# Shared slots of the expert stage gathered ahead of the last own slots

## The chip, the cores and the metric

The kernel runs on one core of one Trainium2 chip. Its engines are TensorE (matmul), VectorE, ScalarE and GpSimd, each with a queue of its own that it works through in order; SyncE issues most plain transfers, GpSimd issues the gathers, whose rows it picks by an index. The metric is the time of one execution in microseconds, as a median of runs.

## The reference

A two-layer network on 256 latent tokens of width 1024 (with 256 context tokens in the first layer). Layer 0 mixes with a state-space scan and attention, layer 1 with a gated MLP; each layer ends with the PEER expert stage, which is what the change touches:

```python
def _peer(h, wq, k1, k2, u_tab, v_tab):
    q = (t @ wq).reshape(n_tok, PEER_HEADS, PEER_DKEY)
    s1 = jnp.einsum('thd,hkd->thk', q[..., :half], k1)
    s2 = jnp.einsum('thd,hkd->thk', q[..., half:], k2)
    ...  # the best 16 of 16384 experts for each of 8 heads: idx, gate
    def expert_block(args):
        tb, ib, gb = args
        act = jax.nn.gelu(jnp.einsum('phkd,pd->phk', jnp.take(u_tab, ib, axis=0), tb), approximate=False)
        return jnp.einsum('phk,phkd->pd', gb * act, jnp.take(v_tab, ib, axis=0))
```

Each token has 128 experts (8 heads x 16). For each it takes the dot product with a row of `u_tab`, a gelu, the gate, and adds that multiple of a row of `v_tab`.

## The kernel before, in words

The 16384 experts are cut into 128 classes of 128. The experts of the first 75 classes (`X`) are computed densely: TensorE multiplies all tokens with every U block (`products`, order "S"), a spread of the gates masks the result `ge`, and then TensorE multiplies `ge` with every V block (order "V", 75 blocks), summing into four PSUM tiles `py`. The blocks come by SyncE into four buffers `wr`, one block of 128 x 1024 floats each. A block of V costs 8 matmuls in the instruction order, which the trace shows as 16 passes.

The experts of the other 53 classes are gathered. The 256 tokens are two tiles (t = 0, 1) of 128. For each tile GpSimd gathers 56 *own slots* (`CAP`): slot s brings, for each of the 128 tokens, one row of 2048 floats (U row and V row, `fetch`, tensor `rows`). VectorE takes the dot product with the token (`dot`, writes `junk` and `act`), ScalarE makes the weight (`weigh`: gelu, then times the gate, `wt`), VectorE adds the weighted V row to `acc`. What tokens have beyond 56 goes to three *shared slots* (`SHARED`): up to 128 pairs of any token and expert each. A shared slot needs two gathers, the expert's row (`in_uv`) and the token's row (`hs`), hence two row buffers; its dot product is taken between them, VectorE makes a 128 x 256 matrix `sc` that carries the weight to the right token, and TensorE multiplies `sc` with the V rows into the same `py` (8 matmuls).

There are six row buffers (`NR`). Two slots stay in `pend` between dot product and accumulation (`LAG`), so up to four gathers are under way. All instructions are written by one Python program: generators for TensorE (`products`), for gathering (`gather`), for the choice and spread (`choose`) and for the end (`ending`) yield to a planner, `schedule`, which runs the one whose engine is free first by the planner's own clock (`clk`). What comes out is a fixed order on each engine; the chip's waits are semaphores between engines. `clock.ready(x)` is the planned time at which `x` is there; `LATE` is how far past it the planner's TensorE clock must be before a shared product is written.

After the last slot, `ending` scales `acc` and adds the residual, `overflow` reads a counter `fi` and branches on it (the branch body, for still longer lists, is not run here), and `finish` (layer 0) or `final` (layer 1) updates x from `py` and `acc`. Every engine goes through the branch. Line 173 is the helper that records all operations, so the profile's groups are told apart by tile names.

Of the kernel before, what the change touches and what calls it, by code (L numbers as in the profile page):

```python
# [33 lines left out]
CAP = 56  # L34
TAKE, TAKES = 24, 3
SHARED = 3
NR = 6
# [14 lines left out]
PACE = 1.0  # L52
NAW = 4
KORDER = (8, 10, 12, 0, 2, 4, 6, 14)
LATE = 6.0
LAG = 2


# [149 lines left out]
def tile_backbone(ctx: ExitStack, tc: tile.TileContext, a: dict, out: bass.AP):  # L208
# [3 lines left out]
    clock = Clock()  # L212
    clk = clock.at
    T, V, S, G, Q = (Engine(e, n, clock) for e, n in ((nc.tensor, "T"), (nc.vector, "V"), (nc.scalar, "S"), (nc.gpsimd, "G"), (nc.sync, "D")))
# [41 lines left out]
    def at(*aps):  # L256

        return lambda: clk["T"] + SLACK >= max(clock.ready(x) for x in aps)
# [1170 lines left out]
    def peer(l, mod, a2, sh2):  # L1429
# [42 lines left out]
        qr, vals, inds = {}, [], []  # L1472
# [152 lines left out]
        def take(t, r_, idx=None, gsl=None):  # L1625

            if idx is None:
                idx, gsl = (x[t][:, TAKE * r_:TAKE * (r_ + 1)] for x in (gidx, gsel))
            tmp = lambda n, dt: q2.tile([P, TAKE], dt, tag=n, name=n)
            ks = [tmp(f"ks{i}", F32) for i in range(3)]  # L1630
            for e in range(0, TAKE, 8):
                for i in range(3):
                    V.max(ks[i][:, e:e + 8], key[t][i])
                for i in range(3):
                    V.match_replace(key[t][i], ks[i][:, e:e + 8], key[t][i], 0.0)
            ki, kb, kc = (tmp(f"k{n}", I32) for n in "ibc")
            for k_, x in ((ki, ks[0]), (kb, ks[1]), (kc, ks[2])):
                V.tensor_copy(k_, x)
            z_, ok, lo = (tmp(n, F32) for n in ("z_", "ok", "lo"))
            V.tensor_scalar(z_, ks[0], 0.0, 65536.0, op0=ALU.is_equal, op1=ALU.mult)  # L1640
            V.tensor_scalar(ok, ks[0], 0.0, None, op0=ALU.is_gt)
            V.tensor_scalar(idx, ki, ROWS - 1, None, op0=ALU.bitwise_and)
            V.tensor_tensor(idx, idx, z_, op=ALU.add)
            V.tensor_scalar(kb, kb, 65535, None, op0=ALU.bitwise_and)
            V.tensor_scalar(kc, kc, 65535, None, op0=ALU.bitwise_and)
            V.tensor_scalar(lo, kc, 1.0 / (GLO * GHI), -32768.0 / (GLO * GHI), op0=ALU.mult, op1=ALU.add)
            V.scalar_tensor_tensor(gsl, kb, 1.0 / GHI, lo, op0=ALU.mult, op1=ALU.add)
            V.tensor_tensor(gsl, gsl, ok, op=ALU.mult)
# [175 lines left out]
        def fetch(rw, idx, src=None, last=(P - X) * P - 1):  # L1824
            G.indirect_dma_start(out=rw, out_offset=None, in_=a[f"uv{l}"] if src is None else src,
                                 in_offset=bass.IndirectOffsetOnAxis(ap=idx, axis=0),
                                 bounds_check=last, oob_is_err=False)

        def weigh(act, g_):
            S.activation(act, act, AF.Gelu)  # L1830
            w = q2.tile([P, 1], F32, tag="wt", name="wt", bufs=4)
            S.activation(w, act, AF.Copy, scale=g_)
            return w
# [65 lines left out]
        def urgent():  # L1899

            if not todo_v:
                return False
            return clk["V"] + SPREAD * todo_v[1] + RUSH > clk["T"] + PTILE * (todo_v[0] + left[0] - 2 * X)

        def gather():
            yield lambda: "sel" in done
            nxt = [clk["T"]]
            todo = [(t, s) for t in range(2) for s in range(CAP)] + [(2, k) for k in range(SHARED)]
            free, work, pend = list(qr["rows"]), [], []
            taken = [EARLY, 0]  # L1910
            head = [0]

            def issue():
                t, s = todo[head[0]]
                if len(free) < (2 if t == 2 else 1):
                    return False
                head[0] += 1
                if t < 2:
                    if s % TAKE == 0 and s // TAKE >= taken[t]:
                        take(t, taken[t])  # L1920
                        taken[t] += 1
                    bufs = [free.pop(0)]
                    fetch(bufs[0], gidx[t][:, s:s + 1])
                else:
                    bufs = [free.pop(0), free.pop(0)]
                    fetch(bufs[0], lidx[:, s:s + 1])
                    fetch(bufs[1][:, 0:D], lidx[:, SHARED + s:SHARED + s + 1], hs, 2 * P - 1)
                work.append((t, s, bufs))
                return True

            def weigh_last():
                if pend and len(pend[-1]) == 5:
                    t, s, bufs, act, g_ = pend[-1]
                    w = weigh(act, g_)
                    if t == 2:
                        sc = q2.tile([P, 2 * P], F32, tag="sc", name="sc")
                        V.tensor_scalar(sc, iotaL[:, :2 * P], spot[:, s, 0:1], w, op0=ALU.is_equal, op1=ALU.mult)
                        w = sc
                    pend[-1] = (t, s, bufs, w)

            def accumulate():
                t, s, bufs, w = pend.pop(0)
                v_ = bufs[0][:, D:2 * D]
                if t == 2:
                    last = s == SHARED - 1 and "pl" in done
                    for t_ in range(2):
                        for n in range(2):
                            mm(py[t_][n], w[:, t_ * P:(t_ + 1) * P], v_[:, n * 512:(n + 1) * 512], False, last)
                    if s == SHARED - 1:
                        done.add("shared")  # L1950
                elif s == 0:
                    V.tensor_scalar(acc[1], v_, w, None, op0=ALU.mult)
                else:
                    V.scalar_tensor_tensor(acc[1], v_, w, acc[1], op0=ALU.mult, op1=ALU.add)
                if t == 0 and s == CAP - 1:
                    Q.dma_start(out=acs, in_=acc[1])
                if t < 2 and s == CAP - 1:
                    done.add(("own", t))
                free.extend(bufs)

            lst = None
            for i in range(NR - LAG):
                issue()
            while work or pend:
                weigh_last()
                if work:
                    t, s, bufs = work.pop(0)
                    if t == 2:
                        yield lambda: "pv" in done
                    yield at(*bufs)  # L1970
                    g_ = lg[:, s, 1:2] if t == 2 else gsel[t][:, s:s + 1]
                    pend.append((t, s, bufs, dot(bufs[1] if t == 2 else h2[t], bufs[0]), g_))
                    if t == 1 and s >= 4:

                        if taken[0] < TAKES or taken[1] < TAKES:
                            t_ = 0 if taken[0] < TAKES else 1
                            take(t_, taken[t_])
                            taken[t_] += 1
                        elif lst is None:
                            lst = listing()  # L1980
                        if lst:
                            next(lst, None)
                if len(pend) > LAG or not work:
                    if len(pend) == 1:
                        weigh_last()
                    if pend[0][0] == 2:
                        yield lambda: clk["T"] >= clock.ready(pend[0][3]) + LATE
                    accumulate()
                while head[0] < len(todo) and len(work) + len(pend) < NR:
                    if todo[head[0]][0] == 2 and todo[head[0]][1] == 0:  # L1990
                        while taken[0] < TAKES or taken[1] < TAKES:
                            t_ = 0 if taken[0] < TAKES else 1
                            take(t_, taken[t_])
                            taken[t_] += 1
                        for _ in lst or listing():
                            pass
                    if not issue():
                        break
                yield
                rest = len(todo) - head[0] + len(work)  # L2000
                nxt[0] = max(nxt[0], clk["T"] - 3.0) + PACE * PTILE * max(0, left[0] - TAIL) / max(1, rest)
                if rest:
                    yield lambda: clk["T"] > nxt[0] and not urgent()
# [170 lines left out]
```

## Time and profile before

| | |
|---|---|
| median of 3 runs | 1990.38 us (1984.54 to 1993.85) |
| profiled execution | 1996.46 us, span 1994.7 us |
| TensorE busy | 1863.6 us |
| VectorE busy | 1369.0 us |
| GpSimd busy | 629.5 us |
| ScalarE busy | 540.2 us |
| mean granted TensorE clock | 0.970 |
| end of the expert stage, layer 0 | first update of x at 1123.83 us |
| end of the expert stage, layer 1 | first update of x at 1980.41 us |

Times in the rows are microseconds from the span's start. In a timeline the columns are start, duration, engine, line, operation, output and inputs, count, and in brackets how long the engine was idle ahead of it and what released it. Rows of several instructions are merged; the start is that of the first. Layer 0 is the first layer, layer 1 the second. `PEld` is TensorE's weight load, which runs beside the matmuls.

### The profile page before, as it was taken

Reading aid. Unit: us, or ns where it says so; the run is one execution under the profiler, and the core shown is the slowest. Engines: PE = TensorE matmul, PEld = TensorE weight load, DVE = VectorE, ACT = ScalarE, POOL = GpSimd, SP = SyncE. Lnnn points to the kernel's source line nnn. Section 1 sums busy time; section 2 is a strip of 40 time slices with the busy share of each in tenths; the row PEclk is TensorE's granted clock in tenths of the full one; section 3 lists DMA queues with packets and bytes.
Section 4 is the critical chain, followed back from the end, with each engine's and each line's share of the span. In section 5 each row is a group of like instructions: output and inputs, shape, how many; then the busy total and the mean of one; then the engine's idle time right before and its main releaser. Section 6 shows DMA issues by size and latency. Waiting matters only on the chain. (4 is left out here: it accounts for less than half of the span.)

```text
span 1994.7 us, 27972 instructions
## 1 busy us (share of the span) xinstructions
PE 1863.6 (93%) x9888; PEld 1539.0 (77%) x9888; DVE 1369.0 (69%) x3376; ACT 540.2 (27%) x1428; POOL 629.5 (32%) x400
## 2 busy tenths in 40 slices
PE   7989999899999999998999698999999999989994
PEld 4666565679988878887878588799888888868773
DVE  4466276546985898778567625479858986876667
ACT  5334344345212222110111354442112221111111
POOL 2324312276010222133322198650112221334222
PEclk9999999899999999999999899999999999989998
DMA  8656766155367989699999474453579885999993
GB/s 314 217 173 220 251 219 212 68 180 169 128 218 276 358 301 365 221 359 367 398 417 395 149 254 147 161 188 128 195 286 362 302 342 220 355 355 400 417 411 128
DMA packets 133064, 529.87 MB, mean 266 GB/s; under 512 B 17941, under 2 KB 18133, under 8 KB 105197
## 3 DMA queue, kind: packets, MB, share of 16 engines
q1 hardware_dynamic: 97440, 301.76, 42.8%
q0 software_dynamic: 34176, 225.07, 28.9%
q8 instruction: 78, 1.28, 0.3%
q10 hardware_dynamic: 1296, 1.16, 0.2%
q14 instruction: 74, 0.61, 0.1%
HBM read 540.28 MB, written 6.91 MB: 274 GB/s over the span
## 5 line engine op out<-in xcount | busy, mean ns | idle before, releaser
L173 POOL DMA_INDIRECT rows<-in_uv,gidx x224 | 270.4, 1207 | 912.9 <-DVE acc L173 657.5
L173 PE MATMUL pb<-wr,ge 128*128 128x256 f32 x2400 | 539.5, 384 | 19.5 <-DMA wr<-in_dn 17.5
L173 PE MATMUL pa<-phf,wr 128*128 128x256 f32 x2400 | 539.1, 385 | 0.0
L173 PEld LDWEIGHTS pb<-wr,ge 128*128 128x128 f32 x2400 | 453.7, 191 | 103.1 <-DMA wr<-in_dn 41.9
L173 PEld LDWEIGHTS pa<-phf,wr 128*128 128x128 f32 x2400 | 458.9, 193 | 61.8
L173 POOL TENSOR_TENSOR whl<-wr,whl 128x1024 fp32r<-128x1024 f32 (+2 forms) x128 | 310.6, 2440 | 306.6 <-ACT whl L173 298.9
L173 DVE SCALAR_TENSOR_TENSOR junk<-rows,h 128x1024 bf16<-128x1024 f32 x224 | 273.8, 1222 | 128.7 <-DMA rows<-in_uv,gidx 128.6
L173 DVE SCALAR_TENSOR_TENSOR acc<-rows,wt,acc 128x1024 f32<-128x1024 f32 x220 | 281.8, 1281 | 0.3 <-ACT wt L173 0.3
L173 ACT ACTIVATE act<-act 128x1 f32<-128x1 f32 x230 | 46.7, 203 | 573.7 <-DVE junk L173 554.8
L173 ACT CAST whl<-wr 128x1024 fp32r<-128x1024 f32 (+2 forms) x136 | 137.3, 1019 | 86.3 <-PE pa L173 37.2
L173 ACT ACTIVATE sg<-pa 128x8 f32<-128x8 f32 (+20 forms) x98 | 26.5, 270 | 278.1 <-PE pa L173 252.3
L173 PE MATMUL pb<-oc,o 128*128 128x75 f16 x1024 | 85.3, 252 | 14.8 <-DVE oc L173 13.6
L173 PE MATMUL pa<-phh,whl 128*128 128x256 f32 x512 | 96.3, 285 | 2.2 <-DVE phf L173 1.5
L173 PEld LDWEIGHTS <-o 128*128 128x128 f16 x1024 | 78.0, 118 | 24.0 <-DVE oc L173 14.8
L173 ACT ACTIVATE ge<-pa 128x256 f32<-128x256 f32 (+18 forms) x146 | 46.9, 321 | 144.9 <-PE pa L173 144.3
L173 PE MATMUL pa<-aw,condT 128*32 128x512 f32 x320 | 78.7, 605 | 6.9 <-DMA aw<-in_ada_w 5.1
L173 PEld LDWEIGHTS pa<-phh,whl 128*128 128x128 f32 x512 | 80.7, 191 | 3.6 <-DVE phf L173 1.9
L173 DVE SCALAR_TENSOR_TENSOR ge<-pb,ge 128x292 f32<-128x292 f32 (+19 forms) x128 | 42.1, 370 | 59.4 <-ACT ge L173 56.5
L173 PE MATMUL pa<-phl,whl 128*128 128x256 f32 x256 | 73.2, 286 | 2.4 <-POOL phl L173 1.3
L173 DVE TENSOR_TENSOR o<-iotaJ,pkT 128x1024 f16<-128x1024 f16 x64 | 43.8, 684 | 36.8 <-PE pb L173 36.8
L173 ACT ACTIVATE wt<-act,gsel 128x1 f32<-128x1 f32 x224 | 66.0, 295 | 7.3
L173 DVE MAX8 ge<-ge 128x8 f32<-128x128 f32 (+1 forms) x192 | 38.4, 254 | 26.0 <-ACT ge L173 25.9
(490 smaller groups left out, 2436.6 us busy)
## 6 DMA issues: line engine op xcount, KB each, us to landing
wr<-in_dn SPq DMA_DIRECT2D x300, 512.0 KB
aw<-in_ada_w SPq DMA_DIRECT2D x164, 256.0 KB
wr<-in_wq SPq DMA_DIRECT2D x32, 512.0 KB
wr<-in_w_out SPq DMA_DIRECT2D x16, 512.0 KB
wr<-in_gm_w_v SPq DMA_DIRECT2D x16, 512.0 KB
wr<-in_gm_w_u SPq DMA_DIRECT2D x16, 512.0 KB
wr<-in_gm_w_out SPq DMA_DIRECT2D x16, 512.0 KB
wr<-in_w_xbc SPq DMA_DIRECT2D x12, 512.0 KB
```

Of the source, the lines that this page charges most:

```text
L173: return f(*args, **kw)
```

## The change

Before, the list of slots is tile 0's 56, tile 1's 56, then the 3 shared ones. After, the 3 shared slots stand ahead of tile 1's last 14 (`AFTER`), that is, ahead of own slots 42 to 55. When a shared slot's turn to be accumulated comes, it goes to a list `lates` and its buffers stay taken; its product is written when TensorE's planned clock is `LATE` = 5.0 (before 6.0) past the planned time of its `sc`, while the loop goes on with other slots. The loop's condition and the count of buffers in use include `lates`.

```diff
-LATE = 6.0
+LATE = 5.0
+AFTER = 14
...
-            todo = [(t, s) for t in range(2) for s in range(CAP)] + [(2, k) for k in range(SHARED)]
-            free, work, pend = list(qr["rows"]), [], []
+            todo = [(t, s) for t in range(2) for s in range(CAP)]
+            todo[2 * CAP - AFTER:2 * CAP - AFTER] = [(2, k) for k in range(SHARED)]
+            free, work, pend, lates = list(qr["rows"]), [], [], []
...
-            def accumulate():
-                t, s, bufs, w = pend.pop(0)
+            def accumulate(t, s, bufs, w):
...
-            while work or pend:
+            while work or pend or lates:
+                if lates and clk["T"] >= clock.ready(lates[0][3]) + LATE:
+                    accumulate(*lates.pop(0))
+                if not work and not pend and lates:
+                    yield lambda: clk["T"] >= clock.ready(lates[0][3]) + LATE
+                    continue
...
-                if len(pend) > LAG or not work:
+                if len(pend) > LAG or not work and pend:
                     if len(pend) == 1:
                         weigh_last()
-                    if pend[0][0] == 2:
-                        yield lambda: clk["T"] >= clock.ready(pend[0][3]) + LATE
-                    accumulate()
-                while head[0] < len(todo) and len(work) + len(pend) < NR:
+                    x = pend.pop(0)
+                    if x[0] == 2:
+                        lates.append(x)
+                    else:
+                        accumulate(*x)
+                while head[0] < len(todo) and len(work) + len(pend) + len(lates) < NR:
```

What this makes of the instruction order is shown for the end of layer 1's expert stage. TensorE before: `wr,ge` are the V blocks (8 rows a block), `rows,sc` the shared products, `fi` the branch.

```order
L173 MATMUL pa<-rhs,cmp 128x2 x6
L173 MATMUL pb<-wr,ge 128x256 x312
L173 MATMUL pb<-rows_13285,sc 128x256 x8
L173 MATMUL pb<-rows_13281,sc 128x256 x8
L173 MATMUL pb<-rows_13283,sc 128x256 x8
L2036 TENSOR_LOAD fi
```

TensorE after, the same place:

```order
L174 MATMUL pa<-rhs,cmp 128x2 x6
L174 MATMUL pb<-wr,ge 128x256 x264
L174 MATMUL pb<-rows_13277,sc 128x256 x8
L174 MATMUL pb<-rows_13279,sc 128x256 x8
L174 MATMUL pb<-wr,ge 128x256 x16
L174 MATMUL pb<-rows_13275,sc 128x256 x8
L174 MATMUL pb<-wr,ge 128x256 x32
L2044 TENSOR_LOAD fi
```

The first two products now stand ahead of the last 6 blocks, the third ahead of the last 4. In layer 0 they stand ahead of the last 9 and the last 7 (`x264`, two products, `x16`, one product, `x56`).

GpSimd before, the end of its gathers in layer 1: `in_uv,gidx` are own slots, `in_uv,lidx` and `hs,lidx` the two gathers of a shared slot.

```order
L173 DMA rows_13283<-in_uv,gidx_11927 128x2048
L173 DMA rows_13284<-in_uv,gidx_11927 128x2048
L173 DMA rows_13285<-in_uv,lidx 128x2048
L173 DMA rows_13286<-hs,lidx 128x1024
L173 DMA rows_13281<-in_uv,lidx 128x2048
L173 DMA rows_13282<-hs,lidx 128x1024
L173 DMA rows_13283<-in_uv,lidx 128x2048
L173 DMA rows_13284<-hs,lidx 128x1024
L2036 TENSOR_LOAD fi
```

GpSimd after, from own slot 41 (buffer 13276) to own slot 47:

```order
L174 DMA rows_13276<-in_uv,gidx_11921 128x2048
L174 DMA rows_13277<-in_uv,lidx 128x2048
L174 DMA rows_13278<-hs,lidx 128x1024
L174 DMA rows_13279<-in_uv,lidx 128x2048
L174 DMA rows_13280<-hs,lidx 128x1024
L174 DMA rows_13275<-in_uv,lidx 128x2048
L174 DMA rows_13276<-hs,lidx 128x1024
L174 DMA rows_13277<-in_uv,gidx_11921 128x2048
L174 DMA rows_13278<-in_uv,gidx_11921 128x2048
L174 DMA rows_13279<-in_uv,gidx_11921 128x2048
L174 DMA rows_13280<-in_uv,gidx_11921 128x2048
L174 DMA rows_13275<-in_uv,gidx_11921 128x2048
```

The three shared slots fill all six buffers, and own slots 42, 44 and 46 are gathered into buffers that TensorE's first, second and third shared product reads (13277, 13279, 13275). Eight more own slots follow.

VectorE after, in the same place, from own slot 41's dot product (`junk,act<-rows_13276,h`) on:

```order
L174 SCALAR_TENSOR_TENSOR junk,act<-rows_13276,h_11913 128x1024
L174 SCALAR_TENSOR_TENSOR acc<-rows_13280,wt,acc 128x1024
L174 SCALAR_TENSOR_TENSOR junk,act<-rows_13277,rows_13278 128x1024
L174 SCALAR_TENSOR_TENSOR acc<-rows_13275,wt,acc 128x1024
L174 TENSOR_SCALAR sc<-iotaL,spot,wt 128x256
L174 SCALAR_TENSOR_TENSOR junk,act<-rows_13279,rows_13280 128x1024
L174 SCALAR_TENSOR_TENSOR acc<-rows_13276,wt,acc 128x1024
L174 TENSOR_SCALAR sc<-iotaL,spot,wt 128x256
L174 SCALAR_TENSOR_TENSOR junk,act<-rows_13275,rows_13276 128x1024
L174 TENSOR_SCALAR sc<-iotaL,spot,wt 128x256
L174 SCALAR_TENSOR_TENSOR junk,act<-rows_13277,h_11913 128x1024
```

The accumulation of own slot 41 (`rows_13276`) stands behind the second shared dot product, and the third shared slot's gathers need the buffer that it frees. Before, the shared dot products came after own slot 55's, and the two passes over `acc` stood ahead of the third.

## Rows read from the trace of the kernel before

**Rows 1.** The page: its span, and busy time of each engine.
```profile
span 1994.7 us, 27972 instructions
PE 1863.6 (93%) x9888; PEld 1539.0 (77%) x9888; DVE 1369.0 (69%) x3376; ACT 540.2 (27%) x1428; POOL 629.5 (32%) x400
```

**Rows 2.** Timeline, layer 1, VectorE's dot products and a weight block's loads.
```profile
1913.45 1.23 DVE L173 SCALAR_TENSOR_TENSOR junk<-rows,h 128x1024 bf16<-128x1024 f32 x1 [1.35 <-DMA rows<-in_uv,gidx]
1917.22 1.23 DVE L173 SCALAR_TENSOR_TENSOR junk<-rows,h 128x1024 bf16<-128x1024 f32 x1 [1.34 <-DMA rows<-in_uv,gidx]
...
1932.40 3.32 PEld L173 LDWEIGHTS pb<-wr,ge 128*128 128x128 f32 x16 [0.41 <-DMA wr<-in_dn]
```

**Rows 3.** Stretches: length; PE, PEld, DVE, ACT, POOL busy; PEclk, DMA share, GB/s.
```profile
1930.00:1940.00 10.00, 9.88 (x45) 7.72 (x43) 6.00 (x8) 1.29 (x5) 2.98 (x3) 1.00 1.02 411
1940.00:1950.00 10.00, 9.38 (x40) 7.31 (x40) 7.11 (x9) 1.49 (x6) 2.02 (x3) 1.00 0.87 333
1950.00:1955.00 5.00, 4.17 (x19) 3.71 (x20) 4.31 (x6) 1.00 (x4) 2.57 (x2) 1.00 0.38 115
...
1960.00:1965.00 5.00, 0.00 (x0) 0.00 (x0) 3.12 (x5) 0.50 (x2) 2.72 (x2) 0.62 0.89 328
```

**Rows 4.** Timeline, the end of layer 1's expert stage.
```profile
1950.69 1.23 DVE L173 SCALAR_TENSOR_TENSOR junk<-rows,h 128x1024 bf16<-128x1024 f32 x1 [0.99 <-DMA rows<-in_uv,gidx]
...
1950.83 5.45 PE L173 MATMUL pb<-wr,ge 128*128 128x256 f32 x24 [1.43 <-DMA wr<-in_dn]
...
1960.06 1.22 DVE L173 SCALAR_TENSOR_TENSOR junk<-rows,h 128x1024 bf16<-128x1024 f32 x1
...
1962.45 0.99 POOL L173 DMA_INDIRECT rows<-hs,lidx  x1 [0.30 <-issue]
1964.37 1.22 DVE L173 SCALAR_TENSOR_TENSOR junk<-rows,rows 128x1024 bf16<-128x1024 f32 x1 [1.89 <-DMA rows<-hs,lidx]
...
1966.72 0.41 DVE L173 TENSOR_SCALAR sc<-iotaL,spot,wt 128x256 f32<-128x256 f32 x1
...
1967.18 12.70 PE L173 MATMUL pb<-rows,sc 128*128 128x256 f32 x48 [10.91 <-DVE sc L173]
...
1968.54 1.23 DVE L173 SCALAR_TENSOR_TENSOR junk<-rows,rows 128x1024 bf16<-128x1024 f32 x1 [1.41 <-DMA rows<-hs,lidx]
...
1971.21 2.48 DVE L173 TENSOR_TENSOR acc<-acc,ge 128x1024 f32<-128x1024 f32 x2
1973.61 1.22 DVE L173 SCALAR_TENSOR_TENSOR junk<-rows,rows 128x1024 bf16<-128x1024 f32 x1
...
1975.43 0.41 DVE L173 TENSOR_SCALAR sc<-iotaL,spot,wt 128x256 f32<-128x256 f32 x1 [0.60 <-ACT wt L173]
...
1975.99 0.15 DVE L173 TENSOR_TENSOR fi<-fi,ff 1x1 int32<-1x1 int32 x1
1979.32 1.28 ACT L173 ACT_TABLE_LOAD   x1 [3.92 <-ACTq L2038]
1980.41 0.69 DVE L173 TENSOR_TENSOR x<-pb,ge 128x512 f32<-128x512 f32 x1 [4.27 <-DMA rows<-hs,lidx]
```

**Rows 5.** Timeline, the end of layer 0's expert stage.
```profile
1058.50 1.23 DVE L173 SCALAR_TENSOR_TENSOR junk<-rows,h 128x1024 bf16<-128x1024 f32 x1 [1.34 <-DMA rows<-in_uv,gidx]
...
1069.68 3.32 PEld L173 LDWEIGHTS pb<-wr,ge 128*128 128x128 f32 x16 [0.44 <-DMA wr<-in_dn]
...
1073.32 1.23 DVE L173 SCALAR_TENSOR_TENSOR junk<-rows,h 128x1024 bf16<-128x1024 f32 x1 [1.04 <-DMA rows<-in_uv,gidx]
...
1077.18 24.04 PEld L173 LDWEIGHTS pb<-wr,ge 128*128 128x128 f32 x112 [0.42 <-DMA wr<-in_dn]
...
1102.86 1.22 DVE L173 SCALAR_TENSOR_TENSOR junk<-rows,h 128x1024 bf16<-128x1024 f32 x1
...
1109.84 13.36 PE L173 MATMUL pb<-rows,sc 128*128 128x256 f32 x48 [8.22 <-DVE sc L173]
...
1123.83 0.69 DVE L173 TENSOR_TENSOR x<-pb,ge 128x512 f32<-128x512 f32 x1 [4.11 <-PE pa L173]
```

## The prediction

> **What bounds the kernel now.** I read the page first, then the timeline of the last 170 us of each layer, the stretch table over the second end, and the instruction order of both programs. The span is 1994.7 us and TensorE is busy for 93% of it [rows 1], so only stretches in which TensorE has nothing to do, or its successor waits, are worth anything. The change touches two: the ends of the two expert stages.
>
> Up to about 45 us before each end, three things run in step. VectorE starts one dot product per own slot, 3.77 us apart (1913.45, 1917.22), each released by the landing of its gather [rows 2]. TensorE starts one block of V weights about as often; its block at 1932.40 takes 3.32 us of loads after a 0.41 us wait for its transfer [rows 2]. A gather (128 x 8 KB) and a weight block (128 x 4 KB) share the transfer engines, which are full: DMA share 1.02 up to 1940 (the 1930 stretch), 0.87 from 1940 to 1950 [rows 3]. Transfers set the pace, and TensorE loses 0.3 to 0.45 us a block to them.
>
> Then the second layer ends like this [rows 4]. TensorE starts its last 24 weight passes at 1950.83 and is through at 1956.28. The last own slot's dot starts at 1960.06 (I number own slots 0 to 55; slot 41, fourteen earlier, starts at 1913.45). Only then come the shared slots: dots at 1964.37, 1968.54, 1973.61. TensorE idles from 1956.28 to 1967.18 and its 48 passes of shared products end at 1979.88; the first update of x starts at 1980.41. VectorE's own work of this end is over at 1976.14. So before, TensorE's late shared products end last, and VectorE has some slack. In the first layer the same: 48 passes from 1109.84, 13.36 us, update at 1123.83 [rows 5].
>
> **The change part by part.** Nothing is added or dropped: 6 shared gathers, 3 dots, 3 `sc` and 24 matmuls a layer are moved ahead of 14 own slots. What counts is who then waits.
>
> *TensorE.* In the new order the first two products stand ahead of the last 6 weight blocks in the second layer (16 + 32 rows, 8 a block), of the last 9 in the first (16 + 56); the third stands two blocks later. One product is 16 passes, like a block: 24.04 us for 112 [rows 5], 3.43 us. [...]
>
> *The ring.* Three shared slots take two buffers each: all six. GpSimd's queue has own slot 42 next, into the first shared slot's buffers, and that instruction waits for TensorE's product; the 13 own gathers queued behind it wait too, VectorE waits for them, and the transfer engines have only weights to carry. Slot 44 waits for the second product, slot 46 for the third. Before, buffers came free from VectorE at its own pace. This wait is new, and the trace of before has no row of it; I time it by what surrounds it.
>
> *Second layer, in the trace's time.* The first shared pair is issued behind own slot 41: its dot comes one whole gather (3.77) and one half-size one (8 of 12 KB a pair, 2.51) after slot 41's: 1913.45 + 6.28 = 1919.7; the second at 1926.0. The third pair needs slot 41's accumulation, which stands behind the second dot; dot and accumulation take 2.34 (1950.69 to 1960.06 is four slots [rows 4]): 1928.3. Two issues of 0.99 with 0.30 ahead of each: 1930.9. A gather issued at 1962.45 with 0.99 was used at 1968.54, 5.1 after its issue [rows 4]: 1936.0, and from a dot to the end of its `sc` (1973.61 to 1975.84) 2.2: 1938.2.
> TensorE reaches the first product at 1932.4, less at most five waits of 0.3 (3.77 less 3.43) that the thinner gather traffic saves: 1930.9. The first two scales are there by then (1964.37 to 1967.13 is 2.8: 1922.5 and 1928.8). Products end at 1934.3 and 1937.8, two blocks 1944.6, third product 1948.1, four blocks 1961.8: TensorE is done 18 us earlier.
> Own slot 42 can be issued at 1934.3 and used about 1941.3. Slot 46 is issued by 1949.4. Its landing takes between 5.1 (the row, half the bytes) and 6.4 (a third of 3.77 more for the second half); I take 5.7: 1955.1. The nine slots behind it run no faster than VectorE's 2.34: 1976.2. The last dot and three accumulations, since two are still owed: four times half of 2.34, 4.7: 1980.9. The two passes over `acc` 2.48, the three small ones on `fi` 0.38, and the branch, which took from 1976.14 to 1979.32 before ScalarE's first instruction behind it [rows 4], 3.2: 1987.0 against 1980.41, **+6.6**. Cover gone: `acc` and the branch lay under TensorE's products before; now they stand behind the last slot.
>
> *First layer.* From slot 41 at 1058.50 the same steps give shared dots at 1064.8 and 1071.1, third pair issued by 1076.0. TensorE's ninth block from the end starts at 1069.68 [rows 5]; the second scale is there at 1073.9, the products end at 1073.1, 1077.3 and, two blocks later, 1087.6; seven blocks end at 1111.6. Slot 42 is free at 1073.1 but stands in GpSimd's queue behind the third pair: issued by 1077.3, used at 1083.0. Nine blocks of weights are not yet consumed, so I take not 2.34 but what this layer's last ten slots took, (1102.86 - 1073.32) / 10 = 2.95 [rows 5]: 13 x 2.95 = 38.4, 1121.4 (slot 46 at 1094.8; its buffer allows 1094.6). With 10.8 behind it 1132.2 against 1123.83, **+8.4**. At 2.34 slot 46's buffer decides: 1094.6 + 9 x 2.34 + 10.8 = 1126.5, +2.7; at 3.77 throughout, +19.
>
> *Rest.* Six of the filler matmuls at the layer border go; they lie under VectorE's x. In the second layer's first half a few own slots and spreads swap places, within VectorE and ScalarE queues that hold the same work: 0, at most 2 either way.
>
> Sum: 6.6 + 8.4 = +15.0. Against the profiled execution's 1996.46 that is 2011.5; that execution lay 6.1 above the median of 1990.38, so I forecast 2005.4. Bounds: the second layer +5 to +9, the first +2.7 to +19, together +7 to +28.
>
> [...]
>
> **The rivals.** *Faster: the ring is not what holds.* If the shared data come and the products run early enough that own slots keep the places they have now (last dots at 1960.06 and 1102.86), adding 4.7 + 6.1 = 10.8 gives 1970.9 and 1113.7: 9.5 and 10.1 less, 1970.8. For it: TensorE's end falls 18 us, DMA share is only 0.38 after 1950 [rows 3], so there is slack in transfers. Against: slot 42's gather stands behind TensorE's product in both layers, and slots 42 to 45 were dotted before that product starts in the trace of before.
> *No change: a cheap restart.* If the third product's place costs nothing and slots 42 to 55 run at 2.34 throughout: 1941.3 + 13 x 2.34 + 10.8 = 1982.5 (+2.1); 1083.0 + 30.4 + 10.8 = 1124.2 (+0.4): 1992.9. It needs the last gathers to come at VectorE's pace beside the weights; the end of the second layer shows that pace, but after the weights.
> *Slower still: the third pair is late.* It is issued last, behind a drained queue; from the point where its scale comes after TensorE's place for it (6 us of margin in the second layer, 1 in the first), each us moves slots 46 to 55 and TensorE one for one. 10 us late in both: +4 and +9 more, about 2018.
>
> **How the numbers follow.** Forecast 0.58, no change 0.20, faster 0.13, slower still 0.09. Half a per cent, 10 us, is about what a measurement can tell. Faster (under 1980): the first rival, 0.13. Same: the second, and the low edge of the forecast: 0.24. Slower: 0.63. The forecast's own range is 1997 to 2018; to leave out no more than two in ten I reach down through the no-change case to 1984.
>
> **What would show it.** Right: TensorE's last matmul some 15 to 18 us earlier than the x update in both layers; a GpSimd gather that waits for TensorE; no own dot for more than 20 us after slot 41's besides the shared three; `fi`, not TensorE, ahead of the x update. Wrong: own dots that go on within 10 us of slot 41's, or an x update released by TensorE.

## The result, and the profile after

The changed kernel takes 2008.52 us (median of 4 runs, 2007.30 to 2010.47), beside 1992.12 us for the kernel before on the same chip (4 runs, 1984.54 to 1996.68). The ratio is 1.010, 95% interval 1.008 to 1.0119: slower by about 1%, 16 us by the medians and 20 by the ratio. A second set of runs (e9 below) gave 1.0122 (1.0095 to 1.015). The forecast was 2005.4, between 1984 and 2018.

The profiled execution took 2009.66 us. Its page shows the same work as [rows 1]: TensorE has 6 passes less (fillers at the layer border).

```profile
span 2007.9 us, 27952 instructions
...
PE 1854.3 (92%) x9882; PEld 1537.7 (77%) x9882; DVE 1373.0 (68%) x3376; ACT 540.2 (27%) x1428; POOL 634.5 (32%) x400
```

**The end of the second layer.** This is the timeline that answers to [rows 2, 4] (columns as there). Slot 41's dot starts at 1921.57. `rows,h` are own slots, `rows,rows` shared ones; GpSimd (POOL) issues the gathers.

```profile
1921.57 1.23 DVE L174 SCALAR_TENSOR_TENSOR junk<-rows,h 128x1024 bf16<-128x1024 f32 x1 [1.35 <-DMA rows<-in_uv,gidx]
...
1927.95 1.22 DVE L174 SCALAR_TENSOR_TENSOR junk<-rows,rows 128x1024 bf16<-128x1024 f32 x1 [3.95 <-DMA rows<-hs,lidx]
...
1930.65 0.99 POOL L174 DMA_INDIRECT rows<-in_uv,lidx  x1 [6.99 <-DVE acc L174]
...
1933.86 7.07 PE L174 MATMUL pb<-rows,sc 128*128 128x256 f32 x32
...
1937.75 1.12 POOL L174 DMA_INDIRECT rows<-in_uv,gidx  x1 [4.81 <-PE pb L174]
...
1941.21 0.99 POOL L174 DMA_INDIRECT rows<-in_uv,gidx  x1 [1.04 <-PE pb L174]
...
1943.62 1.23 DVE L174 SCALAR_TENSOR_TENSOR junk<-rows,h 128x1024 bf16<-128x1024 f32 x1 [5.62 <-DMA rows<-in_uv,gidx]
1947.68 3.62 PE L174 MATMUL pb<-rows,sc 128*128 128x256 f32 x16
...
1951.13 13.98 PE L174 MATMUL pb<-wr,ge 128*128 128x256 f32 x64
...
1951.57 1.98 POOL L174 DMA_INDIRECT rows<-in_uv,gidx  x1 [8.07 <-PE pb L174]
...
1958.94 1.22 DVE L174 SCALAR_TENSOR_TENSOR junk<-rows,h 128x1024 bf16<-128x1024 f32 x1 [1.33 <-DMA rows<-in_uv,gidx]
...
1981.51 1.21 DVE L174 SCALAR_TENSOR_TENSOR junk<-rows,h 128x1024 bf16<-128x1024 f32 x1
1982.65 4.06 DVE L174 SCALAR_TENSOR_TENSOR acc<-rows,wt,acc 128x1024 f32<-128x1024 f32 x3
1986.75 2.48 DVE L174 TENSOR_TENSOR acc<-acc,ge 128x1024 f32<-128x1024 f32 x2
...
1989.38 0.15 DVE L174 TENSOR_TENSOR fi<-fi,ff 1x1 int32<-1x1 int32 x1
...
1993.64 0.69 DVE L174 TENSOR_TENSOR x<-pb,ge 128x512 f32<-128x512 f32 x1 [4.12 <-DVEq L2046]
```

Read it from GpSimd. Its queue has own slot 42 next at 1933 and stands there until TensorE is past its first shared product (1937.75, released by `pb`); twice more it waits like this, 1.04 and 8.07 us, for the second and the third. So slot 42 is dotted at 1943.62, 22.05 us after slot 41, and slot 46 at 1958.94. TensorE is done at 1965.11 (1951.13 + 13.98), 14.8 us earlier than before's 1979.88 (22.9 us earlier, counted from slot 41's dot). But now VectorE is late: last dot at 1981.51, three accumulations, two passes, the counter `fi`, and 4.26 us of branch until x. Before, the two ended together: x started 0.53 us after TensorE's last product, and 4.42 us after `fi`, which is the crossing's own length. Now `fi` alone decides.

The stretches, with the columns of [rows 3], show both halves of it:

```profile
1930.00:1940.00 10.00, 10.00 (x48) 8.81 (x47) 5.01 (x9) 0.99 (x4) 3.94 (x4) 1.00 0.55 187
...
1970.00:1980.00 10.00, 0.00 (x0) 0.00 (x0) 10.00 (x13) 1.99 (x8) 5.19 (x3) 0.50 0.65 202
```

While GpSimd waits, the transfers fall to a share of 0.55 (1.02 before); that capacity is lost. In the second stretch VectorE works without a gap on the slots that should have come in the first, and TensorE stands (granted clock 0.50).

**The end of the first layer** answers to [rows 5].

```profile
1047.81 1.22 DVE L174 SCALAR_TENSOR_TENSOR junk<-rows,h 128x1024 bf16<-128x1024 f32 x1 [1.34 <-DMA rows<-in_uv,gidx]
...
1060.77 7.07 PE L174 MATMUL pb<-rows,sc 128*128 128x256 f32 x32
...
1064.66 0.99 POOL L174 DMA_INDIRECT rows<-in_uv,gidx  x1 [5.50 <-PE pb L174]
...
1068.11 0.99 POOL L174 DMA_INDIRECT rows<-in_uv,gidx  x1 [1.17 <-PE pb L174]
...
1070.28 1.23 DVE L174 SCALAR_TENSOR_TENSOR junk<-rows,h 128x1024 bf16<-128x1024 f32 x1 [1.09 <-DMA rows<-in_uv,gidx]
...
1078.04 24.45 PE L174 MATMUL pb<-wr,ge 128*128 128x256 f32 x112
...
1078.47 1.90 POOL L174 DMA_INDIRECT rows<-in_uv,gidx  x1 [8.08 <-PE pb L174]
...
1111.74 1.21 DVE L174 SCALAR_TENSOR_TENSOR junk<-rows,h 128x1024 bf16<-128x1024 f32 x1
...
1119.61 0.15 DVE L174 TENSOR_TENSOR fi<-fi,ff 1x1 int32<-1x1 int32 x1
...
1128.64 0.69 DVE L174 TENSOR_TENSOR x<-pb,ge 128x512 f32<-128x512 f32 x1 [8.88 <-issue]
```

The same picture, with one surprise at the bottom: from `fi` to x VectorE takes 9.03 us, where the second layer takes 4.26 and before took 4.26 as well, from this row to 1123.83 [rows 5]:

```profile
1119.57 0.15 DVE L173 TENSOR_TENSOR fi<-fi,ff 1x1 int32<-1x1 int32 x1
```

**Where the time went.** Slot 41 comes earlier or later by some us from one execution to the next, so I measure each expert stage from its first own dot product to its first x update, in the one profiled execution of each kernel. The stretch between the layers is 343.3 to 346.2 us in all kernels here but three (e7, e8, e11).

| kernel | first layer | second layer |
|---|---|---|
| before | 507.1 | 512.4 |
| old order kept in that layer (e2, e1) | 507.7 | 508.4 |
| changed, first and second set (after, e9) | 518.6, 518.9 | 520.9, 521.7 |
| changed in that layer alone (e1, e2) | 519.2 | 519.3 |
| changed, 16 memsets more (e5, e10) | 513.0, 512.3 | 517.0, 518.8 |
| token row freed (e3) | 517.4 | 511.0 |
| spread and freed (e4) | 510.0 | 512.6 |
| spread, not freed (e7) | 515.6 | 513.2 |
| products later (e6) | 527.6 | 521.3 |
| last versions (e8, e11) | 511.0, 511.3 | 511.5, 513.3 |

Changed less old is 518.9 - 507.4 = +11.5 in the first layer and 519.5 (mean with e5 and e10) - 510.4 = +9.1 in the second: some +21, which fits the ratios. The two old values of the second layer lie 4 us apart, so +9.1 is good to some us only. In e4, e7, e8 and e11 a wait of 2.6 to 4.2 us falls shortly behind the branch but after the first x update, and so outside these stages (see e5 and e10).

### The profile page after: what moved, and what is told of

Its sections match the earlier page's. It is cut to its first block, busy times and chain, and to the rows that moved or that the text cites. A ratio compares the mean times of both kernels' runs of the same rounds, so it can differ in the third digit from the quotient of the medians.

```text
span 2007.9 us, 27952 instructions
## 1 busy us (share of the span) xinstructions
PE 1854.3 (92%) x9882; PEld 1537.7 (77%) x9882; DVE 1373.0 (68%) x3376; ACT 540.2 (27%) x1428; POOL 634.5 (32%) x400
## 5 line engine op out<-in xcount | busy, mean ns | idle before, releaser
L174 PE MATMUL pb<-wr,ge 128*128 128x256 f32 x2400 | 537.5, 384 | 13.3 <-DMA wr<-in_dn 11.9
L174 ACT ACTIVATE ge<-pa 128x256 f32<-128x256 f32 (+19 forms) x146 | 46.8, 321 | 144.9 <-PE pa L174 144.3
L174 DVE TENSOR_TENSOR oc<-eq,pkT 128x600 f16<-128x600 f16 x128 | 54.5, 467 | 2.2
```

Of the source, the lines that this page charges most:

```text
L174: return f(*args, **kw)
```

## The experiments

Theory: the shared slots put aside hold the ring, own gathers wait on TensorE's fixed place for their products, and the end of the stage hangs on that place. Rivals: the tail alone (accumulation, passes and branch now behind the last slot); the order of code at the branch.

**e1, e2: one layer at a time.**

```diff
-            todo[2 * CAP - AFTER:2 * CAP - AFTER] = [(2, k) for k in range(SHARED)]
+            n_ = 2 * CAP - (0 if l else AFTER)      # e1; e2: (AFTER if l else 0)
+            todo[n_:n_] = [(2, k) for k in range(SHARED)]
```

> The change in the first layer alone; in the second layer the shared slots stand last again. The prediction's own term for the first layer is +8.4: 2000.5 on a kernel before of 1992.1. The two traces give more: from slot 41's dot to the first x update 65.33 us before and 80.8 after, +15.5. If that is a property of the order, the time is 2003 to 2008 and the branch ahead of the x update takes near 9 us again; if the 5 us above the term were one execution's, it is 1999 to 2002.

> The change in the second layer alone. The prediction's term is +6.6 (1998.7), the two traces give +5.1 (1997.2). Both say 1996 to 1999. If instead something outside the two ends costs (the 3.3 us between the layers), this run lies at before's own time plus that, under 1996 or over 2000.

e1: 2004.13 us, ratio 1.0077 (1.0053 to 1.0101), some +15, inside the 2003 to 2008 expected of a property of the order. e2: 2000.66, ratio 1.0054 (1.0034 to 1.0074), some +11, where I had expected 1996 to 1999: a miss, and not by anything between the layers (344.5 us there). Both layers cost more than the prediction's terms. In e2 the gathers ran further ahead of TensorE, and x came 76.6 us after slot 41's dot instead of 72.1. What did not change is the distance from TensorE's first shared product to x; e2's rows:

```profile
1924.29 7.07 PE L174 MATMUL pb<-rows,sc 128*128 128x256 f32 x32
...
1983.95 0.69 DVE L174 TENSOR_TENSOR x<-pb,ge 128x512 f32<-128x512 f32 x1 [4.13 <-DVEq L2047]
```

59.66 us, against 59.78 in the changed kernel (1933.86 to 1993.64). In e5, e9 and e10 it is 59.0, 61.3 and 60.6; in the first layer 67.9, 67.6 and 67.6 (after, e1, e9). So the end follows TensorE's place, not how far ahead of it the gathers ran. That is the ring theory's mark; the tail theory has no reason for it.

**e3: three buffers aside instead of six.**

```diff
-                    pend.append((t, s, bufs, dot(bufs[1] if t == 2 else h2[t], bufs[0]), g_))
+                    pend.append((t, s, bufs[:1], dot(bufs[1] if t == 2 else h2[t], bufs[0]), g_))
+                    free.extend(bufs[1:])
```

> The changed kernel, but the buffer with the tokens' rows goes back to the ring right behind the shared slot's dot product, so that three buffers and not six stand aside. Theory (the ring holds the own gathers): the third pair needs no accumulation of slot 41 any more, own slot 42 is dotted about 20 us after slot 41 in both layers, and the slots behind it find buffers sooner; its order also puts the third product two blocks earlier. I expect 6 to 9 us back in each layer, 1990 to 1997. Rival (the tail: accumulations, passes and branch now stand behind the last slot, and that is the price): the ring is no matter, the time stays at 2005 to 2011.

2000.75 us, ratio 1.0055 (1.0039 to 1.0071): 8 to 12 us better than the changed kernel (2008.52 and, in e9, 2013.24, on other chips), less than I expected. "Who waited for it" of the tile `sc` has GpSimd's waits for TensorE's products (us, times), in the changed kernel, then in e3:

```profile
  POOL rows L174: 29.0, 7
```

```profile
  POOL rows L174: 8.0, 5
```

The second layer is back to the old length (511.0); the first gained only 1.5. The edit did more than free buffers, for the planner's order moved with it. In the second layer the first product now stands ahead of the last 9 blocks, not 6, and the third ahead of 8, not 4; in the first layer it is 10 and 9, not 9 and 7, and TensorE waits 2.67 us for the first `sc` there. Counted from the layer's first own dot, the first product starts at 450.8 us in the second layer (458.0 to 461.1 in the changed kernels) and at 450.5 in the first (450.8 to 451.7); from there to x it takes 60.2 and 66.9 us, much as in the changed kernel. The gain goes with TensorE's earlier place, and so does its absence in the first layer; what three free buffers are worth by themselves this run doesn't show. "The tail alone" is refuted for the second layer: from the last own dot to x it is 12.21 us here and 12.13 in the changed kernel, so the tail is all there, and the loss is gone.

**e4 and e7: the shared slots apart** (ahead of the last 20, 14 and 8 own slots), e4 with e3's edit, e7 without.

```diff
-            todo[2 * CAP - AFTER:2 * CAP - AFTER] = [(2, k) for k in range(SHARED)]
+            for k, n_ in enumerate((20, 14, 8)):
+                todo.insert(2 * CAP - n_ + k, (2, k))
```

> The shared slots no longer stand together: one each ahead of the last 20, 14 and 8 own slots, and the tokens' rows are freed behind the dot, so that at most one or two buffers stand aside at once. Ring theory: no gap of 20 us any more, each shared slot delays the slots behind it by what its gathers take, 2.3 to 6.3 us, so the last own dot comes 7 to 19 us behind before's place (1960.06 and 1102.86) and the tail of 10.8 stands behind it: 1978 to 1990 against 1980.4 in the second layer, 1121 to 1133 against 1123.8 in the first, 1992 plus or minus 8. Tail theory: no better than the changed kernel, 2005 to 2011.

> Shared slots ahead of the last 20, 14 and 8 own slots as in the fourth run, but both buffers stay taken until the product. At most two or three of six buffers stand aside at once. If standing together is what empties the ring, this is as good as the fourth run or little worse: 1993 to 2000. If the tokens' row matters as such, it lies near the changed kernel, 2004 to 2010.

e4: 1994.85 us, ratio 1.0033 (1.0015 to 1.0051), the best order with shared slots ahead. That is what the ring theory gave; the tail theory gave 2005 to 2011, and the tail is all there (12.13 and 12.19 us from the last own dot to x), so the tail alone is refuted for both layers. e7: 2003.94, ratio 1.0062 (1.0042 to 1.0082): my expectation for it was wrong, standing apart is not enough. GpSimd waits 20.1 us for products there (14.8 in e4), and TensorE 13.3 us for `sc` (8.2 in e4). That fits a loss by how many buffers are held for how long, but doesn't show it alone: the first layer is 5.6 us longer than e4's, and there the second and third product also stand one block later; the second layer is 0.6 longer.

**e6: later products.** LATE 12 for 5; no other edit.

> The changed kernel with LATE 12 for 5: the first product keeps its place, the second stands two blocks later, the third five blocks (two it had, three more): its end moves 10.3 us. Ring theory: own slot 46 waits for it (in the second layer from 1958.94 to about 1969, in the first from 1084.84 to about 1095), the slots behind it run at 2.34 us at best, the ends move by 8 to 10 us in the second layer and by 4 to 10 in the first: 2021 to 2029. Rival (the restart alone costs, and it hangs on the first product, or the tail alone costs): no change, 2005 to 2011.

2021.17 us, ratio 1.016 (1.0141 to 1.0179): 8 to 13 us more than the changed kernel, at the low end of what I expected. The rows of e6's second layer:

```profile
1945.81 3.62 PE L174 MATMUL pb<-rows,sc 128*128 128x256 f32 x16
...
1949.27 7.07 PE L174 MATMUL pb<-wr,ge 128*128 128x256 f32 x32
...
1956.17 3.62 PE L174 MATMUL pb<-rows,sc 128*128 128x256 f32 x16
...
1959.63 10.52 PE L174 MATMUL pb<-wr,ge 128*128 128x256 f32 x48
...
1960.06 0.99 POOL L174 DMA_INDIRECT rows<-in_uv,gidx  x1 [7.96 <-PE pb L174]
...
1969.99 3.62 PE L174 MATMUL pb<-rows,sc 128*128 128x256 f32 x16
...
1973.44 10.52 PE L174 MATMUL pb<-wr,ge 128*128 128x256 f32 x48
...
1973.88 0.99 POOL L174 DMA_INDIRECT rows<-in_uv,gidx  x1 [4.39 <-PE pb L174]
...
2011.22 0.69 DVE L174 TENSOR_TENSOR x<-pb,ge 128x512 f32<-128x512 f32 x1 [4.21 <-DVEq L2046]
```

The third product starts 24.18 us after the first (13.82 in the changed kernel), the own gather that needs its buffer (slot 47's, not 46's as I had it) goes out as it ends, and x comes 65.41 us after the first product, 5.6 more; in the first layer 74.34, 6.5 more. Only in the first layer does the first product keep its place as I had expected. There the stage is 527.6 us, 8.7 more than the changed kernel's 518.9, of which 2.2 is TensorE's wait for the first `sc`. In the second layer 8 blocks stand behind the first product (32 + 48 + 48 passes in the rows), not 6; it starts 455.9 us after the layer's first own dot instead of 458.0 to 461.1, and the stage, 521.3 us, is no longer than the changed kernel's. So the first layer shows what a later product costs; the second, where the first product came sooner and the third later, shows no net price.

**e5, e10: 16 instructions ahead of VectorE's code**, e10 beside e9, the unedited changed kernel, on one chip.

```diff
     V.memset(epsc, EPS)
+    spare = cp.tile([P, 1], F32, name="spare")
+    for _ in range(16):
+        nc.vector.memset(spare, 0.0)
```

> The changed kernel with 16 one-column memsets at VectorE's start and no other difference in order, so that everything VectorE runs behind them lies 16 instructions further in its code. In the first layer VectorE took 8.4 to 8.9 us from the branch's counter to the first x update in the three kernels that have the shared slots together there, and 4.0 to 4.3 in the others. Theory (where the code lies decides whether one or two pieces of it must be fetched behind the branch): 4 to 4.4 us now, and the time falls by 4 to 5, to 2002 to 2006. Rival (what goes on around the branch decides: TensorE idle for 18 us, transfers beside it): 8.4 to 9 us again, 2005 to 2011.

> The changed kernel once more, to be set against the next run on the same chip and the same runs of before. The same as so far: 2005 to 2011, 1.008 to 1.012 of before; 8.4 to 9 us from the counter to the first x update in the first layer; the first x update 59 to 60 us behind TensorE's first shared product in the second layer.

> The kernel with 16 memsets more on VectorE again. If the 4.8 us that its first layer lost at the branch hold in all executions, it lies 3 to 6 us under the run before this one; if the branch takes either time by chance, no difference.

e5: 2006.59, ratio 1.0086 (1.0069 to 1.0103), just above the theory's 2002 to 2006 and inside the rival's 2005 to 2011. e9: 2013.24, 1.0122 (1.0095 to 1.015), a little over its expectation. e10: 2006.07, 1.0093 (1.0065 to 1.0121), 7 us under e9, where I had expected 3 to 6. The intervals overlap, so the time alone doesn't decide; the traces do. The first layer's crossing in e10:

```profile
1121.18 0.15 DVE L174 TENSOR_TENSOR fi<-fi,ff 1x1 int32<-1x1 int32 x1
1125.34 0.69 DVE L174 TENSOR_TENSOR x<-pb,ge 128x512 f32<-128x512 f32 x1 [4.01 <-DVEq L2049]
```

and in e9:

```profile
1125.55 0.15 DVE L174 TENSOR_TENSOR fi<-fi,ff 1x1 int32<-1x1 int32 x1
1134.94 0.69 DVE L174 TENSOR_TENSOR x<-pb,ge 128x512 f32<-128x512 f32 x1 [9.24 <-DMA wr<-in_gm_w_v]
```

4.16 against 9.39 us, e5 4.20: the order of work is the same, only the place of the code differs. That refutes the rival. The trace names different releasers for the long wait ("issue" above, a DMA here), so I take none of them for its cause. VectorE's first instruction behind the branch, a semaphore wait, stands 4.0 us after `fi` in the long crossings (after, e1, e3, e6, e9) and 4.0 to 4.2 in the first layer's short ones. The next one waits for a semaphore that was set by 4.1 us, and yet starts only 8.5 to 9.3 us after `fi` in the long crossings. On queue q14, whose kind the profile gives as `instruction`, three packets go 1.8 to 2.7 us after `fi` and three more 5.7 to 8.6, in the first layer of every kernel, so their count doesn't set the length; but in the five long crossings x starts 1.5 to 1.6 us after the last of the six has ended. In the changed kernel VectorE's first instruction, at 4.0 us, stands 1.5 us after the end of the third. From these times I infer that what is missing in the long wait is the instruction itself; no row shows it.

Whether a kernel has the long wait ahead of x is a matter of counting. In the trace's records of VectorE, semaphore instructions included, the branch is number 2141 in the changed kernel and number 2142 before: the new order has one semaphore instruction fewer ahead of it. In all nine kernels that show the long wait it stands behind record 2142. In the five above that is the first instruction behind the branch. In e4, e7, e8 and e11 the branch comes some records earlier and the wait, 2.6 to 4.2 us, falls behind the first, second or third x update, as in e8:

```profile
1125.22 0.69 DVE L174 TENSOR_TENSOR x<-x,ge 128x512 f32<-128x512 f32 x1
1130.09 0.69 DVE L174 TENSOR_TENSOR x<-pb,ge 128x512 f32<-128x512 f32 x1 [4.17 <-issue]
```

Before and e2 have the branch at 2142, e5 and e10 at 2157, and none of them has such a wait. So in these runs the wait comes where the branch stands at record 2141 or a few records ahead of that, and not where it stands at 2142 or 2157. What sets that place no run shows.

**e8, e11: versions meant to beat both**, e3's edit with `(20, 10, 0)` and `(6, 3, 0)` in e4's list; e11 also adds the own slots that are owed ahead of the last shared dot:

```diff
+                    if (t, s) == todo[-1]:
+                        while pend:
+                            x = pend.pop(0)
+                            if x[0] == 2:
+                                lates.append(x)
+                            else:
+                                accumulate(*x)
```

> A version meant to beat both: one shared slot ahead of the last 20 own slots, one ahead of the last 10, the third at the very end as before, tokens' rows freed behind the dot. Two products no longer stand behind TensorE's last block (6.9 us less there at full clock, some 9 at the clock of that stretch), and accumulation, passes and branch lie under the third product again. The transfers still have the same bytes to bring, so the last dot comes at best some 3 to 5 us sooner in each layer: 1980 to 1988 by that. If the transfers alone set the end and the products never did, no change: 1987 to 1993.

> Second version meant to beat both: shared slots ahead of the last 6 and the last 3 own slots and one at the end, tokens' rows freed, and the own slots that wait for accumulation are added before the last shared dot. In the stretch where they now stand VectorE, not the transfers, sets the pace before (2.34 us a slot, DMA share 0.38). Two products no longer stand behind the last shared dot. The last dot comes at 1968 to 1973 by before's rows (1973.61), the passes over acc and the branch stand behind it (9.4): 1977.5 to 1982.5 against 1980.4 in the second layer, the like in the first: 1985 to 1994. If the gathers do not keep up beside the shared pairs there, 1995 to 2000.

e8: 1997.96, ratio 1.0036 (1.0022 to 1.0051); e11: 2002.08, ratio 1.0064 (1.004 to 1.0087). Both expectations failed; neither beats the kernel before. In e11 a product stands ahead of the last three blocks and its `sc` comes too late, so TensorE itself waits in the middle of its weights, in both layers (9.52 and 5.92 us; 9.41 in e8's first layer):

```profile
1956.12 5.49 PE L174 MATMUL pb<-rows,sc 128*128 128x256 f32 x16 [9.52 <-DVE sc L174]
```

The fixed place errs on both sides: too late and the ring stands, too early and TensorE does. e7, e8 and e11 also took 348.7 to 351.2 us between the layers; 3.0 to 4.2 us of that is the wait behind record 2142, which falls after the first x updates there.

## Why the prediction was right

**The mechanism** was the one forecast: all six buffers taken, GpSimd's gather waiting for TensorE three times a layer, 22.05 and 22.47 us between slots 41 and 42 (more than 20 foretold), `fi` ahead of x. One sentence of the forecast was wrong by its own working: TensorE's last matmul should lie 15 to 18 us ahead of x; the steps gave 25.2 and 20.6, and the trace has 28.5 and 26.2 (1128.64 - 1102.49). One premise was wrong too: VectorE had no slack before. x started 4.42 and 4.26 us after `fi` there, as in the kernels where TensorE was done 18 to 30 us before x and the long wait did not come ahead of x (4.2 to 4.5). The forecast saw slack because it ended the branch at ScalarE's first instruction. TensorE's earlier end alone could not have brought x forward by more than some tenths of a us.

**The second layer, +6.6:** from slot 41's dot to x, 73.55 us forecast, 72.07 in the profiled execution, 72.9 to 76.6 in the four others. From TensorE's product to x, 56.1 forecast and 59.78 found: slot 42 came 0.6 sooner than worked out (9.76 after the product's start, not 10.4), slot 46 0.9 later, the slots behind it 22.57 instead of 21.1 (46 to 47 took 3.82), the tail 12.13 instead of 10.8, of which 0.9 is the branch: from the end of `fi` I had 3.2, to ScalarE's first instruction, where VectorE's own row has 4.27 idle [rows 4] and here 4.11. Against that TensorE reached its product sooner: counted from the layer's first own dot 458.0 to 461.1 us, where before's sixth-last block [rows 2] stands at 464.4; I had given it 1.5. As a stage the second layer cost +9.1.

**The first layer, +8.4:** slot 55 came 63.9 us after slot 41 (62.9 forecast), in part by luck: slot 42 came 2.0 us sooner than worked out, and the 13 intervals behind it took 3.1 us more. The step that was mis-sized is the branch in the tail: 3.2 from the end of `fi`, taken from the second layer, 8.88 measured. Without the long wait at the branch (e5, e10) x comes 75.2 and 72.5 us after slot 41's dot, on average 8.2 more than the old order's 65.33 and 65.94 (before, e2), near the forecast term; by stage lengths it is +5.3, 3.1 under it. With it the stage costs +11.5.

**The rivals.** "The ring is not what holds" fell with GpSimd's rows, "no change" with the pace: 13 intervals took 37.9 us in the second layer (2.91 each, not 2.34) and 41.5 in the first. "The third pair late" did not occur: its products start right behind the weights (1947.68), without a wait. The sum, +15.0, stands against 16.4 by the first medians and some 21 by stages and ratios; its sign and cause hold, and what it lacks is about as much as the long wait adds behind the branch (4.8 to 5.2 us: 9.03 in the changed kernel and 9.39 in e9, against 4.20 and 4.16 in e5 and e10), which no row of before shows. The rest cancels by luck: by stages the second layer cost 2.5 us more than forecast, and the first, without the long wait, 3.1 less. Without that wait the whole change costs 0.86 to 0.93% (e5, e10).

**The restart.** The restarted gathers took 4.75 and 4.63 us from the end of the issue to use (1938.87 to 1943.62, 1065.65 to 1070.28), beside others just issued; slot 46's took 5.39 and 4.47. I had taken 5.7, an estimate worked out from the row of 5.1 for half the bytes [rows 4]: 0.3 to 1.2 too much. That row's gather had the same slot's whole gather right ahead of it, issued at 1960.42:

```profile
1960.42 1.73 POOL L173 DMA_INDIRECT rows<-in_uv,lidx  x1 [0.61 <-DVE acc L173]
```

That one landed at 1967.08 and the row's own at 1968.42, so I take its 5.1 to hold some of the other's transfer; that it does is argued, not shown.

## What to carry to other kernels

Work moved ahead holds its buffers until its consumer's place in a fixed order comes. Before moving it, count the buffers that it takes, and follow the next user of each through its queue: here the gathers' queue waited 4.81, 1.04 and 8.07 us for products in the second layer, everything behind them waited too (22.05 us between the dots of slots 41 and 42), and TensorE's saving of 14.8 us became a loss on VectorE, which now was last. Check too how close behind the last engine the next one ends: here VectorE's crossing ended 0.53 us after TensorE's products, so there was next to nothing to save on TensorE alone. Take a branch's price from the engine that is late behind it and from more than one place in the program: here the same order of work crossed in 9.39 us (e9) and, with 16 instructions put in far ahead, in 4.16 (e10).

## What was not expected of the hardware

From the branch's counter to the first x update VectorE takes 4.1 to 4.5 us or 8.5 to 9.4. The long form is a wait behind VectorE's 2142nd record in the trace: one semaphore instruction fewer ahead of the branch goes with it, and 16 instructions put in far ahead took it away (9.39 us in e9, 4.16 in e10).
